# A decoder layer in split fp32 matmuls: silu and gelu as one function, more blocks in seven products, down sums by DMA, the residual held on chip

## The chip, the cores and the metric

The kernel runs on one core of a Trainium2 chip. The metric is the time on the device, in microseconds (us), as the median of several executions. One further execution was recorded by the hardware profiler; all profile lines come from it. The engines are TensorE (PE in the profile, its weight loads PEld), VectorE (DVE), ScalarE (ACT), GpSimd (POOL) and SyncE (SP), whose queue issues nearly all DMAs. Each engine works off its own list of instructions in order and waits on semaphores for the others.

## The reference

One decoder layer on 256 tokens of width 2048, all in fp32:

```python
hn = rmsnorm(h, norm_mix_w)
q, k, v, g_ret, xr, yr, g_a, g_b = split(hn @ w_in)
q, k = rotary(q), rotary(k) * 128**-0.5                    # 8 heads
ret = head_groupnorm(chunkwise_retention(q, k, v), ret_gn_w)
ret_out = silu(g_ret) * ret
hr = rg_lru(causal_dwconv(xr, rnn_conv_w, rnn_conv_b))      # gated linear recurrence
rnn_out = gelu(yr) * hr
merged = sigmoid(g_a) * (ret_out @ w_proj_ret) + sigmoid(g_b) * (rnn_out @ w_proj_rnn)
h = h + merged @ w_mix_out
h = h + memory_cross_attention(rmsnorm(h), rmsnorm(mem), xa_w_q, xa_w_k, xa_w_v, xa_w_o)
up = causal_dwconv(rmsnorm(h) @ ffn_w_up, ffn_conv_w, ffn_conv_b)
gate, val = split(up)                                       # 2 x 5632
h = h + (silu(gate) * val) @ ffn_w_down
return rmsnorm(h, final_norm_w)
```

`gelu` is the tanh form. The weights (some 390 MB) are read once.

## The kernel before

**Products in split fp32.** A factor is held as a high half rounded to the fast fp32r type and a low half, the rest. A product is three matmuls: high by high, low by high, high by low. Activations are held transposed, two slices of 128 features (a "k-pair") to a tile `s`, both halves in it. Weights come as 1 MB tiles `raw`, in the order of use, through `prefetch` (line 275), which keeps `AHEAD = 2` chunks ahead of the product being computed. `weight_parts` (346) makes the halves: ScalarE copies (`hi`, line 351), VectorE subtracts (`lo`, line 352). There are 3 `raw` buffers and 6 buffers each of `hi` and `lo`, a buffer holding a part of two slices by 512 columns.

**Pairs and seven products.** Most products are computed for two blocks of 512 columns at once (`steps_pair`, 477): one chunk is a k-pair of weights for both blocks, 24 matmuls of 128 x 512. In some k-pairs, listed per product (`SEVEN`, `SEVEN_U` and so on), the 2 x 2 x 2 block product is done by Strassen's scheme: seven products instead of eight, 21 matmuls instead of 24. For that `seven_parts` (366) forms four sums of weight blocks on VectorE (line 372) and splits seven parts instead of four, and `sums_of` (444) forms sums of the tokens' tile `ts`. The results lie in several PSUM banks and are put together in `o` tiles by VectorE (lines 525 and 536).

**Order of the work.** The program is written for the Tile layer, which fixes every engine's order from the order of writing and from priorities. `later(n, fn)` (379) puts a piece of work n + 1 chunks further on, so that it stands between the weights' splits of later chunks. `by_dma` (550) turns a result from tokens to features: ScalarE copies it into 16-bit planes (line 558), a transposing DMA on SP turns them, and after `wait` chunks a join (line 571) puts them together and calls what follows. All larger intermediate tiles share 29 buffers of 4 KB per partition (`bp`, line 189).

**The stages**, in the order of the plan (`weight_plan`):
1. The projections of `w_in` with retention (`retain`, 755) between them. The gate's silu is a tanh on ScalarE (846) and a product on VectorE (847); the group norm's factor is multiplied by the token's norm factor (795).
2. Four blocks of the recurrence; `gelu_y` (953) computes the gelu with a square, a tanh and three VectorE passes in each half.
3. The sigmoid gates and `w_proj_rnn`, `w_proj_ret`; `turn_merged` (982) turns the merged rows.
4. `residual` (1014) for `w_mix_out`: four single products of 512 columns, the first three begun together in halves, each added to the rows `hrow` of x. x, the memory rows and the transposed memory are loaded just ahead, and their norms formed by `memory_steps` (1051) during these products. Then `park` (1064) stores `hrow` to DRAM.
5. Cross-attention: keys 0 and 1 as a pair with one block in seven products, then the queries, keys, values. `hrow` is loaded again and `residual` adds `xa_w_o`.
6. Feed-forward: eleven `up` products (1274), each a pair of one gate block and one value block, and three `down` products over 4, 4 and 3 blocks (the down of a group stands after the first up of the next group). Per up, `by_dma` turns both results; `conv` (1165) does the causal convolution (ScalarE line 1170, VectorE line 1172), and `gate_up` (1177) the silu as a tanh, two VectorE products (1182, 1183) and the split. Here the gate's join waits 1 chunk, the value's 3. The first up of each group has two k-pairs in seven products, the others one. `down` (1195) adds its four results to `hrow` on VectorE (line 1199), the last one does it with the final norm.

Of the kernel before, what the change touches and what calls it, by code (L numbers as in the profile page):

```python
# [41 lines left out]
SEVEN = (2, 5)  # L42
SEVEN_O = (3, 5)
SEVEN_U = (4,)
MORE_U = (2, 4)
SEVEN_V = (5,)
# [23 lines left out]

def both(w, c, seven=SEVEN, row=0, nk=NT, apart=BW):

    return w, row, nk, (c, c + apart, seven)


def weight_plan():

    plan = []
    for g in range(2):
        keys = [("w_in", 0, NT, c + g * BW) for c in (O_Q, O_K)]  # L80
        values = [("w_in", 0, NT, O_V + b * BW) for b in range(2)]
        plan += keys + [both("w_in", O_V + 1024, SEVEN_V)] if g else [keys[0], values[0], keys[1], values[1]]
        plan.append(both("w_in", O_G + g * 1024))
# [8 lines left out]
    plan += [both("xa_w_o", 0, SEVEN_O)] + [("xa_w_o", 0, NT, b * BW) for b in (2, 3)]  # L92
    for kind, *a in ff_plan():
        if kind == "down" and sum(a) < NF // 4:
            plan += [both("ffn_w_down", b * BW, SEVEN, a[0] * BW, 4 * a[1]) for b in (0, 2)]
# [36 lines left out]
def by_halves(products):  # L132

    return [c for part in (slice(0, 2), slice(2, 4)) for o in products for c in o[part]]


def weight_stream():
# [7 lines left out]
    i = [c[0][0] for c in out].index("w_mix_out")  # L145
    out[i : i + 3] = [by_halves(out[i : i + 3])]
# [20 lines left out]
def hybrid_layer(  # L167
# [25 lines left out]
    home = ctx.enter_context(tc.tile_pool(name="home", bufs=4, space=bass.MemoryType.DRAM))  # L193
# [508 lines left out]
    half_gn = pb[:, 16:32]  # L702
    dve.tensor_scalar_mul(half_gn, half_gn, 0.5)
# [45 lines left out]
    def split_head(h):  # L749
        f = words[h // 2][:, 2 * (h % 2) : 2 * (h % 2) + 2, :]  # L750
        ret.append(split_cols(f, lambda j: half_gn[:, 2 * h + j : 2 * h + j + 1]))
        if h in SEVEN:
            sums_of(ret[h])

    def retain(g, qr, kr, vs, dec, gates):
# [36 lines left out]
        def normalise():  # L792
            rstd = rsqrt_small(stats[:, :, 1], 8, 1.0, GN_EPS).rearrange("p (h t) -> p h t", t=2)
            for tt in range(2):
                dve.tensor_scalar_mul(rstd[:, :, tt], rstd[:, :, tt], rs0[:, tt : tt + 1])
# [17 lines left out]
            for i in range(2):  # L813
                later(i, lambda i=i: two_heads(i))
# [4 lines left out]
    for g in range(2):  # L819
# [23 lines left out]
        for a in pair("w_in", 0, xs, NT, c, c + BW):  # L843
            t = big([P, 2, BW], s="gate")
            for tt in range(2):
                act.activation(t[:, tt, :], a[:, tt, :], AF.Tanh, scale=half_rs0[:, tt : tt + 1])
            dve.scalar_tensor_tensor(out=a, in0=t, scalar=1.0, in1=a, op0=ALU.add, op1=ALU.mult)
            gates.append(a)
# [31 lines left out]
    K0 = float(np.sqrt(2.0 / np.pi))  # L880
# [43 lines left out]
    for b in range(4):  # L924
# [28 lines left out]
        def gelu_y(f, xr=xr):  # L953
            for pr in range(2):
                y = f[:, 2 * pr : 2 * pr + 2, :]
                y2, th = tmp("y2"), tmp("yt")
                act.activation(y2, y, AF.Square)
                dve.tensor_scalar(out=y2, in0=y2, scalar1=0.044715 * K0, scalar2=K0, op0=ALU.mult, op1=ALU.add)
                dve.tensor_tensor(out=y2, in0=y2, in1=y, op=ALU.mult)
                act.activation(th, y2, AF.Tanh)  # L960
                dve.scalar_tensor_tensor(out=y, in0=th, scalar=1.0, in1=y, op0=ALU.add, op1=ALU.mult)
            for pr in range(2):
# [3 lines left out]
                rnn.append(split_pair(o, 0.5))  # L966
# [13 lines left out]
    merged = []  # L980

    def turn_merged(f):
        for pr in range(2):
            merged.append(split_pair(f[:, 2 * pr : 2 * pr + 2, :], 0.5))

    ts, mb = [], []
    for b in range(2):
        ts.append(tanh_rows(big([P, 2, BW], s="sig"), gemm_n("w_in", 0, xs, NT, O_GB + b * BW)))
        if b == 0:
            for i, k2 in enumerate(SEVEN):  # L990
# [7 lines left out]
    for h in range(HEADS):  # L998
        later(4 + h, lambda h=h: split_head(h))
    ts = []  # L1000
# [344 lines left out]
```

## Time and profile before

| | |
|---|---|
| median of 3 runs (lowest, highest) | 1983.7 us (1983.61, 1985.29) |
| profiled execution | 1982.85 us |
| its span, first to last instruction | 1980.9 us |
| granted TensorE clock | 0.999 |
| busy: PE, DVE, ACT, POOL | 99%, 83%, 70%, 2% of the span |
| DMA: read from HBM, mean rate | 390 MB, 217 GB/s |

In a line of a group, `L352 DVE TENSOR_TENSOR lo<-raw,hi ... x818 | 953.7, 1189 | 249.2 <-ACT hi L351 244.0` reads: line 352, VectorE, what is written from what, how often; together busy 953.7 us, one lasts 1189 ns; VectorE was idle 249.2 us just before these, most of it until ScalarE's `hi` of line 351. In a line of waits stand who waited for whom, the total in us, how often, and the longest. In a table of stretches each line has the stretch, its length, then busy time and instructions of PE, weight loads, DVE, ACT and POOL, the granted clock, the busy share of the DMA engines and GB/s. Matmuls are pipelined: the records of successive ones overlap.

### The profile page before, as it was taken

Reading aid. Unit: us, or ns where it says so; the run is one execution under the profiler, and the core shown is the slowest. Engines: PE = TensorE matmul, PEld = TensorE weight load, DVE = VectorE, ACT = ScalarE, POOL = GpSimd, SP = SyncE. Lnnn points to the kernel's source line nnn. Section 1 sums busy time; section 2 is a strip of 40 time slices with the busy share of each in tenths; the row PEclk is TensorE's granted clock in tenths of the full one; section 3 lists DMA queues with packets and bytes.
Section 4 is the critical chain, followed back from the end, with each engine's and each line's share of the span. In section 5 each row is a group of like instructions: output and inputs, shape, how many; then the busy total and the mean of one; then the engine's idle time right before and its main releaser. Section 6 shows DMA issues by size and latency. Waiting matters only on the chain. (4 is left out here: it accounts for less than half of the span.)

```text
span 1980.9 us, 24128 instructions
## 1 busy us (share of the span) xinstructions
PE 1961.0 (99%) x8798; PEld 1624.5 (82%) x8798; DVE 1644.8 (83%) x2176; ACT 1394.1 (70%) x1714; POOL 31.6 (2%) x25
## 2 busy tenths in 40 slices
PE   9999999999999999999999999999999999999998
PEld 8888888888888888788888888888877888878887
DVE  6887986899898888668888767888889889899786
ACT  6666658989654656697778677787886477774783
POOL 0000001010000000000000000100000000000000
PEclk9999999999999999999999999999999999999999
DMA  8755567665554555897766666577765576665673
GB/s 332 239 213 169 198 245 204 204 223 192 211 211 173 192 212 192 297 308 245 214 222 215 210 216 219 197 230 212 233 203 182 212 232 213 214 201 204 231 252 110
DMA packets 198344, 429.82 MB, mean 217 GB/s; under 512 B 142161, under 2 KB 146769, under 8 KB 153169
## 3 DMA queue, kind: packets, MB, share of 16 engines
q1 hardware_dynamic: 198224, 428.28, 64.5%
q8 instruction: 69, 1.13, 0.2%
q14 instruction: 51, 0.41, 0.1%
HBM read 390.49 MB, written 4.19 MB: 199 GB/s over the span
## 5 line engine op out<-in xcount | busy, mean ns | idle before, releaser
L352 DVE TENSOR_TENSOR lo<-raw,hi 128x1024 fp32r<-128x1024 f32 (+1 forms) x818 | 953.7, 1189 | 249.2 <-ACT hi L351 244.0
L253 PE MATMUL acc<-hi,s 128*128 128x512 f32 (+1 forms) x3632 | 1113.9, 388 | 0.9 <-ACT hi L351 0.8
L351 ACT CAST hi<-raw 128x1024 fp32r<-128x1024 f32 (+1 forms) x818 | 807.8, 1018 | 417.2 <-DMA raw<-in_wall 111.3
L253 PEld LDWEIGHTS acc<-hi,s 128*128 128x128 f32 x3632 | 679.3, 188 | 140.2 <-ACT hi L351 1.5
L253 PE MATMUL acc<-lo,s 128*128 128x512 f32 (+1 forms) x1816 | 704.5, 388 | 3.9 <-DVE lo L352 3.8
L253 PE MATMUL sm<-hi,s 128*128 128x512 f32 x1568 | 482.9, 389 | 0.0
L253 PEld LDWEIGHTS acc<-lo,s 128*128 128x128 f32 x1816 | 341.2, 188 | 76.3 <-DVE lo L352 6.5
L253 PEld LDWEIGHTS sm<-hi,s 128*128 128x128 f32 x1568 | 294.4, 188 | 61.1
L253 PE MATMUL sm<-lo,s 128*128 128x512 f32 x784 | 305.5, 390 | 2.8 <-DVE lo L352 2.7
L571 ACT COPY f<-pt 128x1024 uint16<-128x1024 uint16 x128 | 166.3, 1353 | 14.8 <-DMA pt<-pl 14.6
L253 PEld LDWEIGHTS sm<-lo,s 128*128 128x128 f32 x784 | 147.2, 188 | 34.8 <-DVE lo L352 4.5
L372 DVE TENSOR_TENSOR raw<-raw 128x512 f32<-128x512 f32 x208 | 143.1, 688 | 3.7
L253 PE MATMUL acc<-hi,ts 128*128 128x512 f32 x312 | 96.2, 389 | 0.0
L558 ACT COPY pl<-o 128x1024 uint16<-128x1024 uint16 x68 | 66.7, 1039 | 7.9 <-DVE o L1006 5.2
L253 PEld LDWEIGHTS acc<-hi,ts 128*128 128x128 f32 x312 | 58.5, 188 | 12.2 <-ACT hi L351 0.2
L253 PE MATMUL acc<-lo,ts 128*128 128x512 f32 x156 | 61.5, 394 | 1.7 <-DVE lo L352 1.7
L558 ACT COPY pl<-rows 128x1024 uint16<-128x1024 uint16 x40 | 39.8, 1042 | 21.1 <-DVE rows L584 10.9
L525 DVE TENSOR_TENSOR o<-o,acc 128x512 f32<-128x512 f32 x62 | 42.2, 681 | 0.2
L536 DVE TENSOR_TENSOR o<-o,acc 128x512 f32<-128x512 f32 x62 | 39.6, 680 | 2.9 <-PE acc L253 2.7
L536 DVE TENSOR_TENSOR o<-o,sm 128x512 f32<-128x512 f32 x62 | 40.8, 680 | 0.3
L1172 DVE SCALAR_TENSOR_TENSOR fv<-f,pf,fv 128x255 f32<-128x255 f32 (+1 forms) x88 | 38.7, 479 | 1.7 <-ACT fv L1170 1.5
L525 DVE TENSOR_TENSOR o<-acc,o 128x512 f32<-128x512 f32 x62 | 39.7, 682 | 0.3
(191 smaller groups left out, 1062.6 us busy)
## 6 DMA issues: line engine op xcount, KB each, us to landing
raw<-in_wall SPq DMA_DIRECT2D x352, 1024.0 KB, 4.8
nat<-in_x SPq DMA_DIRECT2D x8, 512.0 KB, 9.1
raw<-in_wall SPq DMA_DIRECT2D x7, 512.0 KB, 6.1
pt<-pl SPq DMA_TRANSPOSE x128, 3.3
nat<-in_mem SPq DMA_DIRECT2D x4, 512.0 KB, 8.7
home<-nat SPq DMA_DIRECT2D x4, 512.0 KB, 6.2
nat<-home SPq DMA_DIRECT2D x4, 512.0 KB, 7.3
xt<-in_x_t SPq DMA_DIRECT2D x3, 512.0 KB, 8.5
```

What stands on the lines that cost most here:

```text
L253: tc.keep_in_program_order(pe.matmul(*a, **k))
L351: act.copy(hi[:, cs], src[:, cs])
L352: dve.tensor_tensor(out=lo[:, cs], in0=src[:, cs], in1=hi[:, cs].bitcast(F32), op=ALU.subtract)
L372: dve.tensor_tensor(out=o, in0=a, in1=b, op=ALU.add)
L525: dve.tensor_tensor(out=o, in0=a, in1=b, op=op)
L536: dve.tensor_tensor(out=o, in0=o, in1=banks[a], op=ALU.add)
L558: act.copy(planes[:, tt], words[:, tt])
L571: act.copy(halves_[:, :, :, cs], turned_[:, :, :, cs])
L1172: dve.scalar_tensor_tensor(out=y[:, s:S], in0=z[:, j, 0 : S - s], scalar=pf[:, 2 - s, t : t + 1], in1=y[:, s:S], op0=ALU.mult, op1=ALU.add,)
```

## The change

- **Silu and gelu.** ScalarE's own silu and tanh-gelu functions take the place of a tanh and the products around it: for retention's gates, in `gelu_y` (one pass over four slices) and in `gate_up`. Factors of one half go away, and so does the product with `rs0` in the group norm.
- **Seven products.** A table `MARKS` lists, for each pair in the plan, the k-pairs that are done in seven products: 62 in all, 52 before. Every up pair now has two, 2 and 5; `w_mix_out`, now two pairs, has one and two; the first key product becomes two single ones with none.
- **Spread gates.** Except for the last up, the value's join waits 4 chunks instead of 3, and convolution and gate are done in two halves, the second one chunk later (`by_two`). Retention's second two heads come one chunk later too.
- **Downs by DMA.** The first two downs are added to `hrow` by accumulating DMAs that POOL issues.
- **Mix-out in pairs.** The rows of x, the memory's squares and its transposed tiles are spread by `later` over the gate and retention projections before it and over the mix-out chunks.
- **Residual on chip.** `hrow` is no longer parked in DRAM.

In the order of the instructions VectorE has 2188 instead of 2174 instructions, ScalarE 1693 instead of 1678 with 20 table loads instead of 11, POOL 38 instead of 30, SP 535 instead of 543, PE 8763 instead of 8793.

```diff
-SEVEN = (2, 5)
-SEVEN_O = (3, 5)
-SEVEN_U = (4,)
-MORE_U = (2, 4)
-SEVEN_V = (5,)
+MARKS = [
+    ((2, 5), (5,), (2, 5)),
+    ((2, 5), (2, 5), (2, 5)),
+    ((2, 5), (2, 5), (2, 5), (2, 5)),
+    ((5,), (3, 5)),
+    ((2, 5), (2, 5), (2, 5), (2, 5)),
+    ((3, 5),),
+    ((2, 5), (2, 5), (2, 5), (2, 5), (2, 5), (2, 5), (2, 5)),
+    ((2, 5), (2, 5), (2, 5), (2, 5), (2, 5), (2, 5)),
+    ((2, 5), (2, 5)),
+]
...
-    plan += [("w_mix_out", 0, NT, b * BW) for b in range(4)]
-    plan += [both("xa_w_k", 0, SEVEN_V), both("xa_w_q", 0), both("xa_w_q", 2 * BW), both("xa_w_k", 2 * BW)]
+    plan += [both("w_mix_out", b * BW) for b in (0, 2)]
+    plan += [("xa_w_k", 0, NT, 0), ("xa_w_k", 0, NT, BW), both("xa_w_q", 0), both("xa_w_q", 2 * BW), both("xa_w_k", 2 * BW)]
...
-            plan.append(both("ffn_w_up", a[0] * BW, MORE_U if plan[-1][0] != "ffn_w_up" else SEVEN_U, apart=FF))
-    return plan
+            plan.append(both("ffn_w_up", a[0] * BW, apart=FF))
+    marks = iter(one for stage in MARKS for one in stage)
+    return [(*p[:3], (*p[3], next(marks)) if isinstance(p[3], tuple) else p[3]) for p in plan]
...
-                dve.tensor_scalar_mul(rstd[:, :, tt], rstd[:, :, tt], rs0[:, tt : tt + 1])
...
-                later(i, lambda i=i: two_heads(i))
+                later(2 * i, lambda i=i: two_heads(i))
...
-                act.activation(t[:, tt, :], a[:, tt, :], AF.Tanh, scale=half_rs0[:, tt : tt + 1])
-            dve.scalar_tensor_tensor(out=a, in0=t, scalar=1.0, in1=a, op0=ALU.add, op1=ALU.mult)
-            gates.append(a)
+                act.activation(t[:, tt, :], a[:, tt, :], AF.Silu, scale=rs0[:, tt : tt + 1])
+            gates.append(t)
...
-            for pr in range(2):
-                y = f[:, 2 * pr : 2 * pr + 2, :]
-                y2, th = tmp("y2"), tmp("yt")
-                act.activation(y2, y, AF.Square)
-                dve.tensor_scalar(out=y2, in0=y2, scalar1=0.044715 * K0, scalar2=K0, op0=ALU.mult, op1=ALU.add)
-                dve.tensor_tensor(out=y2, in0=y2, in1=y, op=ALU.mult)
-                act.activation(th, y2, AF.Tanh)
-                dve.scalar_tensor_tensor(out=y, in0=th, scalar=1.0, in1=y, op0=ALU.add, op1=ALU.mult)
+            act.activation(f, f, AF.Gelu_apprx_tanh)
...
+    ms = Pairs(mem_t, p_mem, 3)
+    ss_mem = sums()[:, :, 0:2]
+    def memory_squares(c):
+        t = load_half(mem, c)
+        later(1, lambda: sum_squares(t, ss_mem, c))
+    def memory_begun():
+        rsms.append(rstd_rows(ss_mem))
+        ms.load(2)
+    marks, more = (c[2] for w, _, _, c in plan if w == "w_mix_out")
     def turn_merged(f):
         for pr in range(2):
             merged.append(split_pair(f[:, 2 * pr : 2 * pr + 2, :], 0.5))
+            if len(merged) - 1 in marks:
+                sums_of(merged[-1])
+            if len(merged) == NT // 2:
+                for i, k2 in enumerate(sorted(set(more) - set(marks))):
+                    later(1 + i, lambda k2=k2: sums_of(merged[k2]))
+            if len(merged) == 2:
+                for k2 in range(NT // 2):
+                    later(1 + 3 * k2, lambda k2=k2: ms[k2])
...
+    for c in range(4):
+        later(6 + 2 * c, lambda c=c: memory_squares(c))
...
+    later(3, memory_begun)
+    for b in range(4):
+        later(8 + b, lambda b=b: hrow.append(load_rows(x, b)))
...
-            if steps:
-                steps(b)
-                if b == 0:
-                    for one in products[:3]:
-                        for _ in range(2):
-                            next(one)
-            elif b == 0:
-                sources += pair(w, 0, st, NT, 0, BW)
+            if b in paired:
+                sources += pair(w, 0, st, NT, b * BW, (b + 1) * BW)
...
-            by_dma(h, lambda f, b=b: turn(f, b, out, wcol), 1 + (b == 1), b == 3 and steps is None)
+            by_dma(h, lambda f, b=b: turn(f, b, out, wcol, marks), 1 + (b % 2 if b in (*paired, *(i + 1 for i in paired)) else 0), b == 3 and w == "xa_w_o")
...
-    def park(h):
-        t = home.tile([P, 2, BW], F32, tag="home", name=nm("home"))
-        sp.dma_start(out=t, in_=h)
-        parked.append(t)
-    ss1 = residual("w_mix_out", merged, h1s, p_xa, memory_steps)
-    for h in hrow:
-        park(h)
+    h1s = []
+    ss1 = residual("w_mix_out", merged, h1s, p_xa, (0, 2), ())
...
-    turned_pair("xa_w_k", ms, 0, rsms[0], keys)
+        turned_rows(a, None, lambda f: split_block(f, osp, marks_of("xa_w_o")))
+    for b in range(2):
+        o = keys[b] = []
+        turned_rows(gemm_n("xa_w_k", 0, ms, NT, b * BW), rsms[0], lambda f, o=o: split_block(f, o))
...
-    for b in range(4):
-        t = big([P, 2, BW], s="nat")
-        sp.dma_start(out=t, in_=parked[b])
-        hrow[b] = t
     h2s = []
-    ss2 = residual("xa_w_o", osp, h2s, p_ffn)
+    ss2 = residual("xa_w_o", osp, h2s, p_ffn, (0,), marks_of("ffn_w_up"))
...
-    def gate_up(gt, vl, hid, seven):
-        for pr in range(2):
-            cs = slice(2 * pr, 2 * pr + 2)
-            th, o = tmp("ft"), tmp("fo")
-            act.activation(th, gt[:, cs, :], AF.Tanh, scale=0.5)
-            dve.scalar_tensor_tensor(out=o, in0=th, scalar=1.0, in1=gt[:, cs, :], op0=ALU.add, op1=ALU.mult)
-            dve.tensor_tensor(out=o, in0=o, in1=vl[:, cs, :], op=ALU.mult)
-            with_sums(hid, seven, o, 0.5)
+    def gate_up(gt, vl, hid, seven, pr):
+        cs = slice(2 * pr, 2 * pr + 2)
+        th, o = tmp("ft"), tmp("fo")
+        act.activation(th, gt[:, cs, :], AF.Silu)
+        dve.tensor_tensor(out=o, in0=th, in1=vl[:, cs, :], op=ALU.mult)
+        with_sums(hid, seven, o)
...
-                dve.tensor_add(hrow[b + i], hrow[b + i], z)
+                pool.dma_start(out=hrow[b + i], in_=z, accum_op=ALU.add)
...
-    def up(b, hid, seven):
+    def up(b, hid, seven, wait):
         gt, vl = (big([P, 4, S], s=a) for a in ("fg", "fv"))
+        def by_two(fn):
+            fn(0)
+            if wait > 3:
+                later(0, lambda: fn(1))
+            else:
+                fn(1)
+        def gate(f):
+            by_two(lambda pr: conv(f, 4 * b, gt, pr))
         def value(f):
-            conv(f, NF + 4 * b, vl)
-            gate_up(gt, vl, hid, seven)
+            def both(pr):
+                conv(f, NF + 4 * b, vl, pr)
+                gate_up(gt, vl, hid, seven, pr)
+            by_two(both)
         two = pair("ffn_w_up", 0, h2s, NT, b * BW, FF + b * BW)
-        for a, then, wait in zip(two, (lambda f: conv(f, 4 * b, gt), value), (1, 3)):
+        for a, then, wait in zip(two, (gate, value), (1, wait)):
...
-            seven = tuple(i - 2 * (b - b0) for i in SEVEN) if b0 < sum(FF_PARTS[:2]) else ()
-            up(b, hid.setdefault(b, []), seven)
+            used = marks_of("ffn_w_down", b0 * BW) if b0 < sum(FF_PARTS[:2]) else ()
+            seven = tuple(i - 2 * (b - b0) for i in used)
+            up(b, hid.setdefault(b, []), seven, 3 if b == NF // 4 - 1 else 4)
```

More of the change, by code (lines that the diff above doesn't have):

```diff
@@ L98, in weight_plan, with marks_of @@
         else:
-            plan.append(both("ffn_w_up", a[0] * BW, MORE_U if plan[-1][0] != "ffn_w_up" else SEVEN_U, apart=FF))
-    return plan
+            plan.append(both("ffn_w_up", a[0] * BW, apart=FF))
+    marks = iter(one for stage in MARKS for one in stage)
+    return [(*p[:3], (*p[3], next(marks)) if isinstance(p[3], tuple) else p[3]) for p in plan]
+def marks_of(w, row=0):
+    return next(c[2] for one, r, _, c in weight_plan() if (one, r) == (w, row) and isinstance(c, tuple))
 def gate_up_at():
@@ L1007, in hybrid_layer, with residual @@
             by_dma(m, turn_merged, 1 + (b + i == 3))
-    hrow = [load_rows(x, c) for c in range(4)]
-    mnat = [load_half(mem, i) for i in range(4)]
-    ms = Pairs(mem_t, p_mem, 3)
-    def residual(w, st, out, wcol, steps=None):
+    def residual(w, st, out, wcol, paired, marks):
         ss = sums()
```

54 lines of the change are left out of this document (18 added, 36 removed).

## The prediction

> **What bounds the kernel now.** Read first: the page's engine totals and slices.
>
> ```profile
> span 1980.9 us, 24128 instructions
> PE 1961.0 (99%) x8798; PEld 1624.5 (82%) x8798; DVE 1644.8 (83%) x2176; ACT 1394.1 (70%) x1714; POOL 31.6 (2%) x25
> PE   9999999999999999999999999999999999999998
> DVE  6887986899898888668888767888889889899786
> ```
>
> TensorE is busy everywhere, VectorE in most slices 80 to 90%. The chain of waits is of no use here: its eleven pieces lie in the last 13 us, all in the final normalisation, which the change leaves alone. So the second reading is by stage: the table of stretches, cut where one matrix product ends and the next begins, counted off in matmuls (186 for a paired product with two blocks in seven products, 189 with one, 96 for a single one). Columns: stretch, its length, busy time with matmuls touched for PE, weight loads, DVE, ACT, POOL, then clock and DMA.
>
> ```profile
> 826.80:850.50 23.70, 22.33 (x97) 17.86 (x96) 11.26 (x12) 12.78 (x16) 0.00 (x0) 1.00 0.98 387
> 850.50:872.30 21.80, 21.80 (x98) 18.04 (x97) 13.66 (x17) 21.80 (x30) 0.70 (x1) 1.00 0.92 267
> 1343.90:1387.20 43.30, 43.09 (x190) 35.40 (x189) 36.64 (x55) 33.66 (x42) 0.00 (x0) 1.00 0.69 196
> 1430.10:1474.40 44.30, 43.45 (x191) 35.25 (x190) 38.30 (x55) 34.44 (x43) 0.00 (x0) 1.00 0.65 198
> 1474.40:1520.70 46.30, 43.28 (x187) 34.50 (x186) 41.54 (x59) 36.48 (x46) 0.00 (x0) 1.00 0.62 203
> 1520.70:1562.90 42.20, 42.20 (x188) 34.92 (x187) 38.74 (x43) 20.71 (x23) 0.00 (x0) 1.00 0.64 236
> 1562.90:1605.10 42.20, 42.20 (x188) 34.96 (x187) 34.77 (x38) 21.54 (x24) 0.00 (x0) 1.00 0.56 204
> 1605.10:1647.90 42.80, 42.80 (x191) 35.45 (x190) 37.71 (x55) 35.05 (x43) 0.00 (x0) 1.00 0.63 194
> 1733.60:1779.80 46.20, 43.30 (x188) 34.52 (x187) 41.44 (x59) 36.37 (x46) 0.00 (x0) 1.00 0.62 204
> ```
>
> An undisturbed paired product takes 42.2 us for 186 matmuls and 42.8 for 189: 0.227 us per matmul. The time is the number of matmuls times this pitch, plus the few places where a product takes longer. Those are: the two first halves of the down products (46.3 and 46.2 against 42.2: 4.1 and 4.0 us too long), two up products (44.3 and 43.3 against 42.8: 1.5 and 0.5) and the second mix-out product (23.7 against 21.8: 1.9). In the feed-forward stage that is 10.1 us. What PE waits for there:
>
> ```profile
> PEld acc L253 <- DVE lo L352: 10.9, 14, 2.1
> PEld sm L253 <- DVE lo L352: 4.5, 4, 1.7
> ACT hi L351 <- DMA raw<-in_wall: 10.9, 4, 7.1
> L352 DVE TENSOR_TENSOR lo<-raw,hi 128x1024 fp32r<-128x1024 f32 (+1 forms) x70 | 82.4, 1190 | 21.3 <-ACT hi L351 21.2
> ```
>
> The first two (waits, whole run) say that PE waits for the low halves of the weights made on VectorE. The third is the same view for 826.8 to 850.5 alone: at mix-out it is a late weight DMA, with the DMA engines 0.98 busy. The fourth is the groups of four successive up products (1301 to 1474): VectorE is not full there, but is idle 21.3 us, 5.3 per product, waiting for ScalarE's high halves. Busy 37.7 plus idle 5.3 is 43.0, the length of a product: VectorE and ScalarE together just keep pace.
>
> **The change part by part.** Seven products in more k-pairs. 62 blocks instead of 52 (ups +8, mix-out +3, the first key product -1), three matmuls less in each: 30 x 0.227 = 6.8 us off PE. All are 512 wide.
>
> ```profile
> L253 PE MATMUL acc<-hi,s 128*128 128x512 f32 x3584 | 1105.2, 390 | 0.9 <-ACT hi L351 0.8
> L352 DVE TENSOR_TENSOR lo<-raw,hi 128x1024 fp32r<-128x1024 f32 x760 | 915.8, 1228 | 240.6 <-ACT hi L351 235.6
> L372 DVE TENSOR_TENSOR raw<-raw 128x512 f32<-128x512 f32 x208 | 143.1, 688 | 3.7
> L352 DVE TENSOR_TENSOR lo<-raw,hi 128x512 fp32r<-128x512 f32 x58 | 39.5, 685 | 8.5 <-ACT hi L351 8.4
> L351 ACT CAST hi<-raw 128x1024 fp32r<-128x1024 f32 x760 | 774.3, 1048 | 400.3 <-PE sm L253 110.0 <-DMA raw<-in_wall 109.4 <-DVE raw L372 102.9
> L351 ACT CAST hi<-raw 128x512 fp32r<-128x512 f32 x58 | 35.4, 616 | 16.9 <-PE acc L253 14.3 <-DMA raw<-in_wall 1.9 <-PE sm L253 0.6
> L1182 DVE SCALAR_TENSOR_TENSOR fo<-ft,fg 128x512 f32<-128x512 f32 x22 | 15.1, 685 | 0.7 <-ACT ft L1181 0.7
> L1199 DVE TENSOR_TENSOR nat<-nat,o 128x1024 f32<-128x1024 f32 x8 | 9.6, 1220 | 0.1
> ```
>
> The group's 390 ns per matmul is not the price: records overlap, and 30 x 0.390 = 11.7 would be too much. The Trainium skill ("Trainium Kernel Development and Optimization", Performance Expectations) calls matmul busy time a bad metric because matmuls are pipelined; 390 ns against a pitch of 227 agrees.
>
> Each block costs VectorE four sums of weights, one more 1024-wide and one 512-wide low half: 4 x 0.688 + 1.228 + 0.685 = 4.7 us, and ScalarE the two high halves (1.05 and 0.62, together 1.66). In an up product the silu takes away two gate products (2 x 0.685 = 1.4). So an up goes from VectorE 37.7 to 41.0 us, while PE falls from 42.8 to 42.2. That is the load of the down product at 1474 (two blocks and the gates of the up before: 41.54 busy, 4.7 idle, 46.3 long). This is the term that decides. Eight ups carry such a load (four before the first down, three before the second, one at the end; the first of each group follows light work), and two downs. Bounds per product: 43.0, if the 3.3 us of added work fill VectorE's idle time (41.0 + 2.0), and 46.3, if the idle time stays (41.0 + 5.3). I take the middle, 44.6, since the sums of weights now stand in the order just where VectorE waits for ScalarE's plane copies, and the second gate half is put one chunk later. Excess over PE: 2.4 per product. Against it stands a lead: six part buffers hold three chunks of 24 matmuls, 16 us, of which some 10 are ahead (estimate). First group, four ups and a down: 12 - 10 = 2; second, 9.6 - 10: none; third none. Add 4 for dips inside a product, as the 0.5 and 1.5 now show at balance. Waits in the feed-forward stage: 6 instead of 10.1, -4.1. Bounds 0 (-10.1) and, at 46.3 per product, 10.5 + 6.4 = 17 (+7).
>
> Downs added by DMAs. Eight sums of 1.22 us leave VectorE, behind which nobody waited; POOL issues eight accumulating DMAs of 512 KB. None is in the trace.
>
> ```profile
> home<-nat SPq DMA_DIRECT2D x4, 512.0 KB, 6.2
> nat<-home SPq DMA_DIRECT2D x4, 512.0 KB, 7.3
> 278.66 3.26 POOL L887 TENSOR_TENSOR rp<-rgw,rp 128x1024 fp32r<-128x1024 f32 x1
> 277.59 5.41 DVE L352 TENSOR_TENSOR lo<-raw,hi 128x1024 fp32r<-128x1024 f32 x2
> ```
>
> Nearest are the plain copies, 6.2 and 7.3 us; between 6 and three times that, 22. The next reader of the sum is the same block's next down, over 250 us later, or the final rows, and only then would it cost; the tile that is freed later is needed again a product (42 us) later. POOL's queue holds nothing else until the final powers. Cost 0.
>
> Residual kept on chip. Four stores and four loads of 512 KB leave SP's queue, which nobody waited for. Four of 29 large buffers stay taken through attention. Counted in the instruction order, 28 are live at the worst point of the queries, as many as before at the end of this gate product, which shows no wait:
>
> ```profile
> 551.50:593.70 42.20, 42.20 (x188) 34.94 (x187) 38.36 (x48) 22.42 (x26) 0.00 (x0) 1.00 0.56 207
> 678.00:720.20 42.20, 42.20 (x188) 34.96 (x187) 40.63 (x56) 27.72 (x38) 0.00 (x0) 1.00 0.59 215
> pt<-pl SPq DMA_TRANSPOSE x128, 3.3
> ```
>
> Cost 0.
>
> Mix-out in pairs, its rows and the memory loaded during the products ahead. The 1.9 us for the late weights go. But the second pair has two blocks beside the turning of the first (counted at the rows' prices: VectorE 42 us, ScalarE 36 in 42.2), and the memory squares fall into the last retention projection. Between 0 and 4; I take 2. Sum 0.
>
> Silu and gelu.
>
> ```profile
> L917 ACT ACT_TABLE_LOAD x4 | 5.1, 1283 | 0.1
> L960 ACT ACTIVATE yt<-y 128x512 f32<-128x512 f32 x8 | 5.1, 632 | 3.6 <-DVE y L959 3.6
> L957 ACT ACTIVATE y<-f 128x512 f32<-128x512 f32 x8 | 5.0, 624 | 0.1
> L847 DVE SCALAR_TENSOR_TENSOR o<-gate,o 128x1024 f32<-128x1024 f32 x4 | 4.7, 1222 | 2.0 <-ACT gate L846 2.0
> L917 ACT ACTIVATE tt<-tt 128x1024 f32<-128x1024 f32 x4 | 4.2, 1061 | 1.8 <-DVE tt L909 1.8
> 309.00:466.00 157.00, 156.78 (x726) 130.93 (x725) 135.86 (x180) 138.67 (x183) 13.90 (x7) 1.00 0.67 211
> ```
>
> Gelu replaces 16 passes (10.1 us) by four 1024-wide ones (at the square root's 1.06: 4.2) on ScalarE, and VectorE loses four gate products of 1.22 and 24 passes of the gelu. The program has 20 table loads instead of 11: 9 x 1.283 = 11.5 us, five of them in this stretch. ScalarE there +0.5 in 138.7 of 157. PE loses 0.2 us there, so nothing is gained on VectorE's side and nothing lost: 0. If ScalarE's cover (18 us) were gone, the loads would cost 6.4.
>
> Sum: -6.8 - 4.1 + 0 = -10.9. The profiled execution took 1982.85 (span 1980.9 and 1.95 around it): 1972. The median, 1983.7, is 0.85 higher: **1973**.
>
> **Rivals.** (1) VectorE and ScalarE become the bound of the ups, and it gets slower. For it: the 46.3 of the down at 1474, twice seen, with the same load; against: the new order of that load. At 46.3 per product and a lead of 8 instead of 10: 12.5 + 8.4 = 21 us of waits, +10.8 - 6.8 = +4: 1988. It decides from about 45.5 us per loaded product.
> (2) The waits go entirely: VectorE's idle 5.3 is filled and the spread gates leave no dips: -6.8 - 10.1 - 1.9 = 1965. For it: the gate product at 678, where VectorE is busy 40.63 of 42.2 us and PE loses nothing; against: ScalarE there has 27.7 us of work, in an up some 36.7 (35.05 and 1.66 for the block).
> (3) Accumulating DMAs hold VectorE up. The two rows above show it for POOL work: two low halves took 5.41 us instead of 2 x 1.23 beside POOL's sum, 3 us lost. Eight times that, two in each of four products with 3.5 and 7.4 us spare (38.74 and 34.77 of 42.2): some 5 us in all: 1978. The Trainium skill ("SBUF — State Buffer", the two separate sides, the "DVE blocks DMA" trap) has the opposite order: descriptors of GpSimd's DMAs wait for VectorE; then only the landing is late, which 250 us cover. No run here has shown either.
> (4) The kept residual makes buffers short in attention, and joins wait: four waits of 3 to 5 us, a transpose of 3.3 and what follows it: +15 on the forecast: 1988. Against it the count of 28.
>
> **How the numbers follow.** Chances: forecast (1967 to 1979) 0.58, (1) 0.18, (2) 0.12, (3) 0.04, (4) 0.08. What a measurement here can tell from no change is 0.2%, 4 us: faster is below 1979.7, slower above 1987.7. Faster: 0.58 less an edge of 0.02, plus (2) and (3): 0.72. Same: the edge, 0.06 of (1), 0.02 of (4): 0.10. Slower: 0.18. The range, 1964 to 1990, takes in (2) and (1) with 1 to 2 us by which runs of one kernel differ, and leaves out their far sides. The likeliest case alone: 1967 to 1979.
>
> **What would show it.** Right: 186 matmuls in every up, each lasting 42.2 to 44.6; VectorE's idle time before low halves well under 5 us per product; the first halves of the downs under 44; no late weights at mix-out. Wrong: ups of 46 us with PE waiting for low halves; low halves of 2 to 5 us beside POOL; plane copies or joins in attention waiting for buffers; a second mix-out pair over 46 us.

## The result and the profile after

The changed kernel takes 1973.53 us (median of four executions, 1971.99 to 1976.45), the kernel before on the same chip 1984.49 (1983.61 to 1985.34): a ratio of 0.9947, 95% interval 0.9929 to 0.9964. It is faster by half a per cent. One execution each of runs 3 and 12 below ran throughout at a low granted clock (3304 us at 0.56, 2164 us at 0.85) and is left out of their medians. The page of the changed kernel's profiled execution begins:

```profile
span 1970.2 us, 24139 instructions
PE 1953.4 (99%) x8768; PEld 1618.3 (82%) x8768; DVE 1653.1 (84%) x2190; ACT 1417.8 (72%) x1729; POOL 31.9 (2%) x33
DVE  6887987888798887997888767789999889998786
```

PE has the 30 matmuls fewer, the span is 10.7 us shorter, and VectorE is 8 us busier. The table of stretches, cut at the same places as in the prediction (retention's last projection, the two mix-out pairs, then the feed-forward products that answer to those shown of before; columns as there):

```profile
761.70:805.20 43.50, 42.67 (x188) 34.79 (x187) 37.32 (x46) 31.72 (x38) 0.00 (x0) 1.00 0.72 243
805.20:848.00 42.80, 42.80 (x190) 35.44 (x189) 38.83 (x50) 31.76 (x39) 0.00 (x0) 1.00 0.73 245
848.00:892.70 44.70, 42.77 (x187) 34.76 (x186) 41.66 (x56) 35.66 (x51) 0.00 (x0) 1.00 0.66 214
1299.80:1342.00 42.20, 42.20 (x188) 34.96 (x187) 37.19 (x54) 37.58 (x46) 0.00 (x0) 1.00 0.62 197
1342.00:1384.10 42.10, 42.10 (x187) 34.88 (x186) 38.89 (x57) 35.67 (x44) 0.00 (x0) 1.00 0.69 222
1384.10:1426.90 42.80, 42.49 (x188) 34.85 (x187) 41.40 (x59) 36.86 (x46) 0.00 (x0) 1.00 0.65 221
1426.90:1470.60 43.70, 42.59 (x187) 34.66 (x186) 41.64 (x60) 38.33 (x48) 0.00 (x0) 1.00 0.67 217
1470.60:1514.60 44.00, 43.39 (x188) 34.54 (x187) 40.74 (x58) 35.39 (x44) 0.00 (x0) 1.00 0.69 215
1514.60:1556.70 42.10, 42.10 (x187) 34.89 (x186) 38.35 (x44) 20.80 (x23) 2.61 (x3) 1.00 0.77 258
1683.20:1725.40 42.20, 42.20 (x188) 34.92 (x187) 40.65 (x59) 36.06 (x45) 0.00 (x0) 1.00 0.70 224
1725.40:1769.00 43.60, 42.59 (x187) 34.74 (x186) 40.49 (x57) 36.38 (x46) 0.00 (x0) 1.00 0.71 217
1928.20:1945.20 17.00, 16.77 (x74) 13.40 (x73) 13.41 (x16) 10.46 (x16) 0.00 (x0) 1.00 0.36 124
```

Call the excess of the feed-forward the sum over its products of what they last beyond 42.2 us (two blocks), 42.8 (one block) or 16.3 (a single product of the last down). Before it was 10.1 us. Now it is 0.6 + 1.5 + 1.8 + 1.4 + 0.7 = 6.0: the fourth and fifth up (1384, 1427), the first halves of the downs (1471, 1725) and the third product of the last down (1928). At mix-out the excess is 1.3 at 762 and 2.5 at 848; before it was 1.9 for the late weights and 0.5 in retention's last projection:

```profile
762.30:805.00 42.70, 42.43 (x187) 34.83 (x186) 36.76 (x43) 30.04 (x33) 0.00 (x0) 1.00 0.59 194
```

The whole balance is: matmuls -6.8, feed-forward -4.1, mix-out +1.4, attention -0.6 (PE was idle 1.1 us in its products of values, now 0.6), the single product at 370 -0.5: -10.6 of the -10.7.

Two lines on what VectorE and PE wait for, from the waits of the whole run and from the groups of the four ups between 1299.8 and 1470.6:

```profile
PEld acc L257 <- DVE lo L356: 10.6, 14, 1.5
L356 DVE TENSOR_TENSOR lo<-raw,hi 128x1024 fp32r<-128x1024 f32 x77 | 87.6, 1168 | 11.1 <-ACT hi L355 11.0
```

PE still waits for low halves. But VectorE's idle time ahead of them fell from 21.3 us to 11.1 in four ups, 2.8 per product: the added work has filled half of it.

The accumulating DMAs, from the view of their source line and from the DMA issues:

```profile
L1183 POOL DMA_DIRECT2D nat<-o x8: 859/867/1071, 1515.3 to 1813.1; - x8
DMA to landing us min/median/max: 5.3/6.3/11.2
nat<-o POOLq DMA_DIRECT2D x8, 512.0 KB, 6.3
```

POOL needs 0.87 us in the median to issue one, and it lands after 6.3 us in the median, 11.2 at most. Nobody is listed as waiting for them.

### The profile page after: what moved, and what is told of

Its sections match the earlier page's. It is cut to its first block, busy times and chain, and to the rows that moved or that the text cites. A ratio compares the mean times of both kernels' runs of the same rounds, so it can differ in the third digit from the quotient of the medians.

```text
span 1970.2 us, 24139 instructions
## 1 busy us (share of the span) xinstructions
PE 1953.4 (99%) x8768; PEld 1618.3 (82%) x8768; DVE 1653.1 (84%) x2190; ACT 1417.8 (72%) x1729; POOL 31.9 (2%) x33
## 4 chain that ended last, share of the span: by engine, by line
PE 81%; DVE 10%; ACT 5%; issue 2%; DMA 2%; SPq 0%; POOL 0%; POOLq 0%; ACTq 0%; DVEq 0%
PE acc L257 56%; PE sm L257 24%; DVE lo L356 4%; ACT f L575 2%; ACT hi L355 2%; DMA raw<-in_wall 2%; DVE raw L376 1%; DVE fv L1158 1%; DVE o L540 1%; DVE o L529 1%; DVE s L596 0%; DMA pt<-pl 0%; DVE fo L1167 0%; ACT fg L1156 0%; ACT pl L562 0%
## 5 line engine op out<-in xcount | busy, mean ns | idle before, releaser
L356 DVE TENSOR_TENSOR lo<-raw,hi 128x1024 fp32r<-128x1024 f32 (+1 forms) x838 | 969.4, 1184 | 231.8 <-ACT hi L355 223.2
L355 ACT CAST hi<-raw 128x1024 fp32r<-128x1024 f32 (+1 forms) x838 | 824.3, 1014 | 391.0 <-DVE raw L376 108.0
L257 PE MATMUL acc<-hi,s 128*128 128x512 f32 (+1 forms) x3548 | 1087.3, 388 | 0.7 <-ACT hi L355 0.3
L257 PEld LDWEIGHTS acc<-hi,s 128*128 128x128 f32 x3548 | 663.2, 188 | 137.2 <-ACT hi L355 0.8
L257 PE MATMUL acc<-lo,s 128*128 128x512 f32 (+1 forms) x1774 | 687.4, 388 | 0.0
L376 DVE TENSOR_TENSOR raw<-raw 128x512 f32<-128x512 f32 x248 | 171.2, 690 | 4.3
L257 PE MATMUL acc<-hi,ts 128*128 128x512 f32 x372 | 115.1, 390 | 1.2 <-ACT hi L355 1.2
L257 PEld LDWEIGHTS acc<-hi,ts 128*128 128x128 f32 x372 | 69.5, 188 | 16.6 <-ACT hi L355 2.6
L257 PE MATMUL acc<-lo,ts 128*128 128x512 f32 x186 | 73.8, 397 | 5.2 <-DVE lo L356 5.1
L257 PEld LDWEIGHTS acc<-lo,ts 128*128 128x128 f32 x186 | 34.9, 188 | 17.0 <-DVE lo L356 10.2
L529 DVE TENSOR_TENSOR o<-o,acc 128x512 f32<-128x512 f32 x64 | 43.7, 683 | 0.1
## 6 DMA issues: line engine op xcount, KB each, us to landing
nat<-in_x SPq DMA_DIRECT2D x8, 512.0 KB, 10.6
```

Source lines behind the costliest of these rows:

```text
L257: tc.keep_in_program_order(pe.matmul(*a, **k))
L355: act.copy(hi[:, cs], src[:, cs])
L356: dve.tensor_tensor(out=lo[:, cs], in0=src[:, cs], in1=hi[:, cs].bitcast(F32), op=ALU.subtract)
L376: dve.tensor_tensor(out=o, in0=a, in1=b, op=ALU.add)
L529: dve.tensor_tensor(out=o, in0=a, in1=b, op=op)
```

## The experiments

Each is set against the kernel before on the same chip, which took 1981.9 to 1982.7 us there; kernels of different chips are compared by their ratios.

**1. Only the blocks.** The kernel before, with two k-pairs in seven products in every up:

```diff
-SEVEN_U = (4,)
-MORE_U = (2, 4)
+SEVEN_U = (2, 5)
+MORE_U = (2, 5)
```

> The kernel before with k-pairs 2 and 5 in seven products in all eleven ups (14 blocks become 22), nothing else. Matmuls: 24 fewer, 24 x 0.227 = 5.4 us off TensorE. Theory A (TensorE's pitch sets the time as long as VectorE and ScalarE together keep pace, and the silu and the spread gates are what lets them): without these VectorE has 37.7 + 4.7 = 42.4 us of work in an up of 42.2, so waits for low halves in the feed-forward stage grow from 10 us to 15 to 30 us: 1984 to 1998 us, no gain or a loss. Rival B (blocks pay wherever they are put, the waits do not depend on them): 1984 - 5.4 = 1979 us, waits still 10 us.

Measured: 1991.09 us against 1982.19, ratio 1.0046 (1.0031 to 1.0061). It is slower, by 8.9 us. Stretches of two ups before the first down, of that down's first half, and of an up before the second down:

```profile
1342.70:1387.30 44.60, 42.84 (x188) 34.80 (x187) 41.29 (x61) 35.78 (x44) 0.00 (x0) 1.00 0.71 213
1387.30:1432.80 45.50, 42.83 (x187) 34.60 (x186) 43.30 (x62) 37.53 (x47) 0.00 (x0) 1.00 0.65 216
1477.60:1522.10 44.50, 42.79 (x188) 34.76 (x187) 41.86 (x59) 35.55 (x44) 0.00 (x0) 1.00 0.67 213
1648.60:1695.60 47.00, 43.25 (x187) 34.49 (x186) 43.09 (x61) 36.84 (x46) 0.00 (x0) 1.00 0.68 207
```

VectorE alone now has 41 to 43 us of work in products that need 42.2, and they last 44.5 to 47.0. The excess of the feed-forward is 24.1 us. 24 matmuls less are -5.4, 14.0 of excess more make +8.6, near the 8.9 measured. What rival (1) described does occur, but where the silu and the spread gates are missing.

**2. All but the ups' blocks.** The changed kernel, with the ups' old lists of k-pairs (two in the very first up and in the first after a down, one in the others):

```diff
-    ((2, 5), (2, 5), (2, 5), (2, 5), (2, 5), (2, 5), (2, 5)),
-    ((2, 5), (2, 5), (2, 5), (2, 5), (2, 5), (2, 5)),
-    ((2, 5), (2, 5)),
+    ((2, 4), (4,), (4,), (4,), (4,), (2, 5), (2, 5)),
+    ((2, 4), (4,), (4,), (4,), (2, 5), (2, 5)),
+    ((2, 4), (4,)),
```

> The changed kernel with the ups' blocks of before (14 instead of 22). Theory A: 24 matmuls more, +5.4 us, of which the feed-forward waits (5.6 us now) give back 2 to 5: 1974 to 1977 us. Rival B: +5.4: 1979 us, waits unchanged. Rival C (VectorE is the bound of the ups, so the added blocks brought nothing): 1973 us or less.

Measured: 1973.2 us, ratio 0.9959 (0.9944 to 0.9973), not to be told from the changed kernel; it is rival C's time rather than theory A's. An up and the down's first half in the table of stretches:

```profile
1387.90:1430.70 42.80, 42.80 (x190) 35.48 (x189) 36.39 (x51) 34.93 (x44) 0.00 (x0) 1.00 0.70 236
1473.60:1515.80 42.20, 42.20 (x188) 34.93 (x187) 38.17 (x56) 35.56 (x44) 0.00 (x0) 1.00 0.70 223
```

Every feed-forward product lasts its minimum; the excess is 0. So without the blocks all 10.1 us of waits go, and the blocks then buy 5.4 us of matmuls with 6.0 us of new waits. In the ups, taken together, they bring nothing.

**3. No spreading.** The changed kernel, with the value's join after 3 chunks, convolution and gate in one piece:

```diff
-            up(b, hid.setdefault(b, []), seven, 3 if b == NF // 4 - 1 else 4)
+            up(b, hid.setdefault(b, []), seven, 3)
```

> The changed kernel with the value's join after 3 chunks and convolution and gate in one piece, as before. Theory A: the dips come back, the first halves of the downs at 46 us again and waits in the last up of each group: feed-forward waits 10 to 16 instead of 5.6: 1978 to 1984 us. Rival (the order does not matter, only the sum of work): 1973.5 us, waits 5.6.

Measured: 1986.12 us, ratio 1.0019 (1.001 to 1.0029): the gain is gone. The fifth up, in one stretch and then in three of 4 us:

```profile
1429.60:1476.40 46.80, 44.54 (x188) 35.84 (x187) 42.58 (x60) 38.34 (x49) 0.00 (x0) 0.96 0.63 201
...
1461.60:1465.60 4.00, 1.74 (x8) 1.17 (x7) 4.00 (x7) 2.75 (x5) 0.00 (x0) 0.98 0.62 246
1465.60:1469.60 4.00, 4.00 (x13) 3.12 (x12) 4.00 (x6) 2.17 (x3) 0.00 (x0) 0.60 0.61 213
1469.60:1473.60 4.00, 4.00 (x19) 3.31 (x18) 3.36 (x5) 2.37 (x3) 0.00 (x0) 1.00 0.74 264
```

VectorE is busy without a break while PE waits 2.3 us (4.00 less 1.74), then the granted clock falls to 0.60 for a slice: 13 matmuls instead of 19. The feed-forward's excess is 18.4 us, above the 10 to 16 expected. That is 12.4 more than in the changed kernel, and the span is 12.4 longer too (1982.6 against 1970.2).

**4. The down sums on VectorE.**

```diff
-                pool.dma_start(out=hrow[b + i], in_=z, accum_op=ALU.add)
+                dve.tensor_add(hrow[b + i], hrow[b + i], z)
```

> The changed kernel with the eight down sums on VectorE again instead of accumulating DMAs. Theory A: they fall into the second halves of the downs and the first up of a group, where VectorE has 3 us or more to spare: 1973 to 1974.5 us, waits 5.6 to 7. Rival: VectorE is full in the whole stage and 8 x 1.22 = 9.8 us come back: 1983 us.

Measured: 1974.65 us, ratio 0.9963 (0.9949 to 0.9977). The second half of the first down:

```profile
1516.60:1559.40 42.80, 42.49 (x187) 34.86 (x186) 40.99 (x46) 20.71 (x24) 0.00 (x0) 1.00 0.61 233
```

It lasts 42.8 instead of 42.2, and the other second half too: the sums make waits of 1.2 us in all, less than the medians can show.

**5. The changed kernel again,** on the chip of the following three.

> The changed kernel itself, on the chip of the three others, as their measure: about 0.9947 of the kernel before, feed-forward waits of 4 to 7 us.

Measured: 1974.82 us (1970.14 to 1975.94), ratio 0.996 (0.9947 to 0.9973). The feed-forward's excess is 5.6 us, close to the 6.0. The second mix-out pair lasts 46.7 us here instead of 44.7; the last section says why.

**6. The old gate in the ups.** The silu as a tanh and two VectorE products, the rest as in the changed kernel:

```diff
-        act.activation(th, gt[:, cs, :], AF.Silu)
-        dve.tensor_tensor(out=o, in0=th, in1=vl[:, cs, :], op=ALU.mult)
-        with_sums(hid, seven, o)
+        act.activation(th, gt[:, cs, :], AF.Tanh, scale=0.5)
+        dve.scalar_tensor_tensor(out=o, in0=th, scalar=1.0, in1=gt[:, cs, :], op0=ALU.add, op1=ALU.mult)
+        dve.tensor_tensor(out=o, in0=o, in1=vl[:, cs, :], op=ALU.mult)
+        with_sums(hid, seven, o, 0.5)
```

> The changed kernel with the ups' silu as a tanh and a product on VectorE, as before (1.37 us more on VectorE per up, one table load less there); all else kept. Theory A (VectorE's work counts, because the loaded ups leave it 1 to 2 us): ten loaded products, 13.7 us of work with hardly a lead to hide it: feed-forward waits 14 to 19 instead of 5.7, 8 to 13 us slower than the changed kernel. Rival D (the order alone removed the waits, the work does not matter): within 2 us of the changed kernel.

Measured: 1985.64 us, ratio 1.0019 (1.001 to 1.0029). The fourth up:

```profile
1385.30:1434.50 49.20, 44.75 (x188) 36.52 (x187) 47.32 (x67) 38.27 (x48) 0.00 (x0) 0.93 0.68 199
```

VectorE is busy 47.3 of 49.2 us. The feed-forward's excess is 17.8 us. Silu and spreading are each worth some 12 us once the ups carry two blocks (17.8 and 18.4 of excess, against 5.6 and 6.0), slow matmuls after the longest waits included; without either the blocks cost more than they save.

**7. One block fewer at mix-out.**

```diff
-    ((5,), (3, 5)),
+    ((5,), (5,)),
```

> The changed kernel with one block in seven products in the second mix-out pair instead of two. Theory A (the second block overfills VectorE and ScalarE there): the wait of 2.5 us in that pair goes, three matmuls cost 0.7: 1.5 to 2 us faster than the changed kernel. Rival E (that wait is a late weight DMA beside the memory's loads, 5.6 us of ScalarE's idle time there): the wait stays, 0.7 us slower.

Measured: 1974.02 us, ratio 0.9963 (0.9949 to 0.9977). The second pair:

```profile
849.20:894.10 44.90, 43.42 (x190) 35.32 (x189) 35.99 (x48) 34.92 (x49) 0.00 (x0) 1.00 0.63 205
```

VectorE has 36.0 us of work instead of 41.7, and the pair still lasts 2.1 us over 42.8. So the sum of work in the product is not what makes it wait. Where PE waits, from 870 to 882, the view of waits has, among others:

```profile
PEld acc L257 <- ACT hi L355: 1.2, 1, 1.2
ACT hi L355 <- DVE raw L376: 1.9, 2, 1.5
```

This is the k-pair still done in seven products (5): PE waits first for ScalarE's high halves, and these wait for VectorE's sums of weights. In the changed kernel it waits at the same k-pair. A second pair with no block at all was not run.

**8. Fewer blocks where VectorE is full.** One block instead of two in the fourth, fifth and ninth up and in the second mix-out pair:

```diff
-    ((5,), (3, 5)),
+    ((5,), (5,)),
...
-    ((2, 5), (2, 5), (2, 5), (2, 5), (2, 5), (2, 5), (2, 5)),
-    ((2, 5), (2, 5), (2, 5), (2, 5), (2, 5), (2, 5)),
+    ((2, 5), (2, 5), (2, 5), (5,), (5,), (2, 5), (2, 5)),
+    ((2, 5), (2, 5), (2, 5), (5,), (2, 5), (2, 5)),
```

> The changed kernel with one block instead of two in the last two ups before the first down, in the last up before the second, and in the second mix-out pair: 12 matmuls more, +2.7 us. Theory A (blocks pay as long as the lead lasts and cost as much as they save once it is used up): the feed-forward waits of 5.7 us fall to 0 to 1, the mix-out wait of 2.5 goes: 3 to 5 us faster than the changed kernel, near 1969. Rival: the waits sit in the downs whatever the ups do: up to 2 us slower.

Measured: 1969.89 us (1969.12 to 1971.93), ratio 0.9943 (0.9928 to 0.9958), beside 1974.82 for the changed kernel on the same chip. The only feed-forward product with an excess to speak of:

```profile
1724.40:1768.30 43.90, 42.68 (x187) 34.60 (x186) 39.85 (x56) 35.90 (x45) 0.00 (x0) 1.00 0.66 216
```

The excess is 1.9 us instead of 5.6, more than the 0 to 1 expected, for 9 matmuls more in the ups (2.0 us); at mix-out, with 3 more, the second pair still lasts 2.1 us too long. The spans of the two profiled executions are 4.6 us apart: 1.7 of that is the feed-forward, 1.8 the mix-out pair (46.7 in run 5, 44.9 here). This kernel has the lower median; the two intervals overlap, so that it is the better one is likely and not shown.

**9. Old blocks and no spreading:** 2 and 3 together; in the feed-forward the silu and the DMA sums are left of the change, and that the value's convolution and gate are written half by half.

> The changed kernel with the ups' blocks of before and without the spread gates: of the three edits of the ups only the silu is left (1.37 us less VectorE work per up, sums by DMA as well). It splits the 10 us of waits that vanish between silu and spread. If the work on VectorE sets the waits: about 2 us of waits left in the feed-forward stage, 1975 us. If the dips set them, from a value joined and gated in one piece beside the down's blocks: 6 to 9 us left, 1980 to 1983 us.

Measured: 1975.26 us, ratio 0.9956 (0.9941 to 0.9971). An up and the first down's first half:

```profile
1430.50:1473.40 42.90, 42.90 (x191) 35.49 (x191) 37.74 (x52) 35.64 (x45) 0.00 (x0) 1.00 0.72 231
1473.40:1516.50 43.10, 42.49 (x188) 34.82 (x187) 38.30 (x55) 34.32 (x43) 0.87 (x1) 1.00 0.60 186
```

The excess is 1.9 us: of the 10.1, silu and DMA sums (with the value's order by halves) remove 8.2, and the spreading the last 1.9. By run 4 the sums are worth about 1.2 beside loaded ups; the silu alone was not run.

**10. The work around mix-out spread.** Kernel 8, with the join of the first pair's second block two chunks later and its squares three:

```diff
-            by_dma(h, lambda f, b=b: turn(f, b, out, wcol, marks), 1 + (b % 2 ...), ...)
+            late = 3 if w == "w_mix_out" and b < 2 else 1
+            by_dma(h, lambda f, b=b: turn(f, b, out, wcol, marks), 1 + late * (b % 2 ...), ...)
...
-                later(2 + b, lambda h=h, b=b: squares(h, ss, b))
+                later((5 if w == "w_mix_out" else 2) + b, lambda h=h, b=b: squares(h, ss, b))
```

> The version with fewer blocks where VectorE is full, and in the mix-out pairs the join of the first pair's second half two chunks later and the squares of its rows three chunks later. Theory F (the wait of 2 us in the second mix-out pair is a burst on ScalarE: four joins, squares, splits of rows and memory in 15 us, with two high halves among them, and late weights only follow from it): that wait falls under 1 us, 1968 us. Rival E (late weight DMAs, whatever ScalarE does): the wait stays at 2 us, 1970 us.

Measured: 1971.02 us, ratio 0.9935 (0.9919 to 0.9951). The second pair:

```profile
849.70:892.50 42.80, 42.80 (x190) 35.47 (x189) 35.84 (x46) 33.75 (x48) 0.00 (x0) 1.00 0.66 212
```

The wait, 2.1 us in kernel 8, is gone, so it came from the crowding of the first pair's turning and squares around the k-pair in seven products. Late weights, rival E, it was not: ScalarE still waits for them, without PE:

```profile
ACT hi L355 <- DMA raw<-in_wall: 4.8, 3, 1.8
```

The time is that of kernel 8, not the 1968 expected: in this execution the first product of all, the one at 187 us, and the second keys and first values lasted 1.0 to 2.0 us too long each, in that of kernel 8 0.3 to 1.7, and so little can't be told apart by medians.

**11. The residual parked again:** four stores after mix-out and four loads ahead of the output projection.

```diff
+    parked = []
+    for h in hrow:
+        t = home.tile([P, 2, BW], F32, tag="home", name=nm("home"))
+        sp.dma_start(out=t, in_=h)
+        parked.append(t)
...
+    for b in range(4):
+        t = big([P, 2, BW], s="nat")
+        sp.dma_start(out=t, in_=parked[b])
+        hrow[b] = t
```

> The changed kernel with the residual stored to DRAM after mix-out and loaded before the output projection, as before. Theory A: hidden, 0 within 1 us of the changed kernel (1974). Rival: stores and loads of 4 MB lie in the way of weights, or the four buffers that they free remove waits in attention: 1 us or more either way, seen in attention's waits of 1.1 us.

Measured: 1971.06 us, ratio 0.994 (0.9923 to 0.9957), as the changed kernel. Keeping the residual is worth nothing that can be measured.

**12. The old gelu.** Square, tanh and three VectorE passes as before, in the changed kernel.

```diff
-            act.activation(f, f, AF.Gelu_apprx_tanh)
+            for pr in range(2):
+                y = f[:, 2 * pr : 2 * pr + 2, :]
+                y2, th = tmp("y2"), tmp("yt")
+                act.activation(y2, y, AF.Square)
...
+                dve.scalar_tensor_tensor(out=y, in0=th, scalar=1.0, in1=y, op0=ALU.add, op1=ALU.mult)
```

> The changed kernel with the recurrence's gelu by square, tanh and three VectorE passes in each half, as before, and 15 table loads instead of 20. Theory A: TensorE loses nothing in that stage either way: 0 within 1 us of the changed kernel (1974). Rival: ScalarE, up to 0.99 busy in single products there, sets the pace, and the five loads of 6.4 us show as waits that now go or come.

Measured: 1975.94 us (five executions, 1972.16 to 1979.38), ratio 0.9959 (0.9944 to 0.9974). The first product of the recurrence's stretch that differs, in this kernel and then in the changed one:

```profile
371.10:399.70 28.60, 26.53 (x122) 22.10 (x121) 23.50 (x30) 24.39 (x37) 1.35 (x2) 0.94 0.82 252
```

```profile
369.40:394.10 24.70, 24.70 (x122) 20.89 (x121) 21.40 (x22) 24.36 (x34) 3.77 (x2) 1.00 0.82 256
```

With the old gelu this product is 3.9 us longer, in the longest of the five executions. PE waits there for a tile of the recurrence that ScalarE writes:

```profile
PE sm L257 <- ACT ti L902: 2.1, 1, 2.1
```

In the kernel before, with the same gelu, it was 0.5 us too long. Of the 3.9 here some 1.7 is the lower clock (0.94 over 28.6 us); why PE waits so long at this place and not at its like is not shown. The medians don't separate 0 from 4 us.

## Why the prediction was right, and where it was not

**The sum.** 1973 was forecast, 1973.5 measured; the span fell by 10.7 us, against a sum of -10.9.

**Matmuls, -6.8.** As worked out: 30 fewer, and every undisturbed pair with two blocks lasts 42.2.

**Waits of the feed-forward, 6 instead of 10.1.** The total is what was forecast, the parts are not. The load of 41.0 on VectorE was right late in each group (41.4 and 41.6 at 1384 and 1427, 40.7 at 1683; the 37.2 and 38.9 at 1300 and 1342 are what VectorE got done there while its lead shrank). The step "I take the middle, 44.6" can't be judged by the length of the ups (42.2 to 43.7), for as long as the lead lasts it hides the price. But the lead can be counted off in the trace, low halves against matmuls: the time from the end of a product's first low half to the product's beginning. These are the first low halves of the up at 1299.8 and, five loaded products later, of the down's second half at 1514.6 (start, length):

```profile
1290.39 1.23 DVE L356 TENSOR_TENSOR lo<-raw,hi 128x1024 fp32r<-128x1024 f32 x1 [1.42 <-ACT hi L355]
1512.83 1.23 DVE L356 TENSOR_TENSOR lo<-raw,hi 128x1024 fp32r<-128x1024 f32 x1
```

The first ends 8.2 us ahead, the second 0.5. So 7.7 us of lead were used up and 3.9 waited: 11.6 in five products, 2.3 each, close to the 2.4 of the sum. In the second group the lead falls from 9.7 to 1.5, with 1.4 us of waits: 9.6 in four products, 2.4 each. The price was right in the mean; the lead of "some 10" was too large by some 2 us in each group, and so they waited 3.9 and 1.4 where 2 and 0 were forecast. Against that, of the 4 for dips hardly any is left: 0.7 in the last group. That these two errors cancel and the total comes out is luck.

**What the sum did not say.** It put -6.8 on the blocks and -4.1 on the waits, as if they were two gains. Runs 2 and 9 divide it otherwise: silu and DMA sums alone take 8.2 us from the waits, spreading the rest, and the blocks of the ups then give 5.4 and take 6.0. Run 1 has the blocks without that room: 14.0 more of waits. The blocks that pay are those that the lead still carries, in the ups at 1300 and 1342 and their like after the next down; run 8 keeps these.

**Rival (1)** was the right danger: 44.5 to 47.0 us per product in run 1, up to 46.8 and 49.2 in runs 3 and 6. It had 0.18; each of two parts of the change, missing, would have brought it about. The argument against it, "the new order of that load", is what run 3 confirms: the order is worth 12.4 us. **Rival (2)** holds for the feed-forward with the ups' old blocks only (run 2, no excess). **Rival (3)** falls: the DMAs were issued in 0.87 us beside a VectorE busy 38.35 of 42.1 us (1514.6), and no VectorE instruction between their issue and landing was more than some 2% longer than its group's median. The Trainium skill ("SBUF — State Buffer", the "DVE blocks DMA" trap) would have had the descriptors wait while VectorE runs in its two-port mode; a median landing of 6.3 us, between the plain copies' 6.2 and 7.3, shows nothing of it; why one took 11.2 is open. Whether VectorE's operations here run in that mode no run shows. **Rival (4)** falls with run 11 and an attention that waits 0.6 us less than before.

**Mix-out, 0.** It cost +1.4 us: 0.6 more in the pair than the late weights took before, 0.8 in retention's last projection. Not the memory's squares fall there (they lie in the gate product at 677, which shows no wait), but four splits of its transposed tiles, 1.8 us of ScalarE; that these make the 0.8 is likely and not shown. The wait of PE for late weights went, as predicted (ScalarE still waited 5.6 us for them there, 10.9 before), and a wait of 2.5 us came, near the 2 taken. But the wait's reason was another: the prediction named the two blocks beside VectorE's 42 us (41.66 measured). Run 7 takes a block away and the wait stays; run 10 spreads the turning and the squares and it goes. The count of work per product was right and did not explain it: work that bunches inside a product is not seen in its sum. In run 5 the pair even lasted 46.7, over the 46 named as a sign of being wrong.

**Downs by DMA, residual, gelu, table loads: 0.** Runs 4 and 11 agree within what can be measured, run 12 leaves 0 to 4 us open for the gelu in its new surroundings.

## What to carry to other kernels

Before trading matmuls for work on other engines, count the busy and the idle time of those engines product by product: three matmuls (0.68 us) for 4.7 us of VectorE cost no wait only as long as VectorE was ahead. Each loaded product used up some 2.4 us of a lead of 8 to 10, so that waits began with the third or fourth, and from then on a block cost more than it saved (run 8: three fewer in the ups, 2.0 us of matmuls against 3.7 of waits). A product that runs at full pace behind such a lead does not show its price; the lead does. Take work off the loaded engine first and look at the waits again; here that alone took away 8.2 of 10.1 us of them. A full sum per product tells of a lack, an even one does not tell of a bunch inside: shift the pieces and look.

## What was not expected of the hardware

A wait of PE of some 2 us can cost more than its own length. The second mix-out pair of the changed kernel lasted 44.7 us in one execution and 46.7 in another. In the longer one, in stretches of 1 us:

```profile
878.00:879.00 1.00, 0.48 (x3) 0.06 (x1) 0.97 (x2) 0.36 (x1) 0.00 (x0) 1.00 0.00 0
879.00:880.00 1.00, 0.26 (x1) 0.26 (x2) 0.97 (x3) 0.69 (x1) 0.00 (x0) 1.00 0.00 0
880.00:881.00 1.00, 0.47 (x2) 0.04 (x1) 1.00 (x2) 0.90 (x1) 0.00 (x0) 1.00 0.00 0
881.00:882.00 1.00, 0.80 (x2) 0.71 (x3) 0.97 (x2) 1.00 (x3) 0.00 (x0) 0.68 0.02 8
882.00:883.00 1.00, 1.00 (x4) 0.71 (x4) 1.00 (x2) 1.00 (x3) 0.00 (x0) 0.50 0.00 0
883.00:884.00 1.00, 1.00 (x4) 0.81 (x3) 1.00 (x2) 1.00 (x3) 0.00 (x0) 0.50 1.01 147
884.00:885.00 1.00, 1.00 (x5) 0.76 (x4) 1.00 (x2) 1.00 (x2) 0.00 (x0) 0.62 0.67 270
```

PE is idle 2.0 us in 878 to 882, and then the granted clock (the third number from the end) is 0.50 for 3.4 us, with four matmuls touched per us. The length beyond 42.2 splits into 2.05 us of waiting (46.70 less PE's busy 44.65) and 2.45 of longer matmul time. Of that the lower clock makes about 1.7 (estimate: what is missing from 1.00 in the last four slices, 0.32 + 0.50 + 0.50 + 0.38); most of the rest the shorter execution has too (PE busy 42.77, 0.57 over 42.2). A fall of the same 3.4 us stands in five other traces, after idle times of 2.3 us (run 3), 1.8 (run 4), 1.8 (run 6, at mix-out), 2.0 (run 9) and 2.1 (run 12), counted within 3.4 us; with the 4.45 us of run 6's fourth up it lasts 6.8. Waits as long passed without one: 1.9 us in the shorter execution, 2.1 in run 11, 2.25 in run 3 and 2.46 just after run 6's second down began:

```profile
1734.00:1738.00 4.00, 1.54 (x7) 0.98 (x6) 3.80 (x6) 2.60 (x5) 0.00 (x0) 1.00 0.00 0
```

So the length of the wait does not decide it alone; what does, no run here shows. The Trainium skill ("TensorE: Matmul & The Clock Gate", What's actually happening) has the clock halved after an idle window of about 3.4 us; here 1.8 to 2.3 us of idle time were enough, and in runs 3, 5 and 12 matmuls were running again when the clock fell. No term of the prediction had this: it priced a wait at its length.
